# Half-row loads of x, weights split two steps ahead, and taps inside the pairs in a one-layer hybrid trunk

## The chip, the core and the metric

One core of one Trainium2 chip runs the kernel. The metric is the device time of one execution in microseconds; lower is better. A core has a matrix engine (TensorE, in the rows PE, with its weight loads as PEld), VectorE (DVE), ScalarE (ACT), GpSimd (POOL) and SyncE (SP); DMAs are issued here from the queues of SP, GpSimd and ScalarE.

## What is computed

One layer over 1024 tokens of width 1024, all in float32:

```python
h = rms_norm(x, norm_g)
z = einsum('bsd,de->bse', h, w_in)                     # 1024 -> 11 * 1024
u = gelu(z_u); v = layer_norm(gelu(z_v))
br_a = gmlp_spatial_gate(u, v, w_s, b_s) * silu(z_ga)  # per chunk of 128 tokens
c = causal_depthwise_conv(z_a * sigmoid(z_b), conv_w)  # 31 taps
br_b = silu(layer_norm(c)) * silu(z_gb)
att = memory_cross_attention(z_q, rms_norm(mem), w_kv) # 4 heads, 256 memory tokens
br_c = att * silu(z_gc)
proj = einsum('bsnw,nwd->bsnd', [br_a, br_b, br_c], w_branch)
merged = sum over n of sigmoid(z_merge)[n] * proj[n]
out = rms_norm(x + einsum('bsd,de->bse', merged, w_out), final_norm_g)
```

## The kernel before

Every product is made of three: each operand is split into a high part (a cast on ScalarE, `A.copy`, L74) and a low part (a subtraction on VectorE, L75), and high*high, high*low and low*high are summed. So a weight costs TensorE time only after both have run on it. Tiles come from pools: `slots` holds 39 buffers of 4 KB per partition, the tag `op` six buffers for operands (`NOP`), `raw` three for weights as loaded.

A planner puts the instructions of each engine in an order, from the program's order and readiness; what goes through `keep` (and `raw_load` with `pin`) stays behind the instruction written before it on its engine. All loads of the opening go through `sload` (L177), which is kept so, on SP's queue.

The stages, in order of time:

- **Memory keys** (L258 to L310): eight chunks of the key weights (`kload`, three in flight), with the gains of the memory rows. `x_load(k)` (L190) brings the transposed row tile k of x, 512 KB, into its slot, all eight between chunk 2 here and chunk 0 of the next stage; `x_gain` (L244) reads only its first half. `diagonals` (L112) spreads per-token factors onto diagonal tiles that `spread` multiplies by ones; it takes `op` buffers.
- **Memory values** (L336 to L370): eight chunks (`v_load`), product L352. At chunk 1, `xt_load` brings four (`NXT`) token-major tiles of x, at chunks 5 and 6 `squares` sums one each and loads another. The values go to DRAM through GpSimd's queue (`vdram`).
- **The v projection** (L387 to L437), product L400: 16 weight chunks, loaded with `raw_load(wv[...], True)`; `squares(6)` stands behind chunk 0; `x_norm` and `combine` prepare both halves of x in spare time.
- **Pairs** (L687 to L716): for p of 4 and ten blocks i of the input projection, `pair` (L454) makes two output tiles out of seven half-size products L446 (Strassen-Winograd), each 12 instructions of 512 columns. Its operands are made by `operand`. The last two products of a pair are written as `pend` and run inside the next. Behind each pair `pump(PUMP[i])` writes 3 to 8 taps of the depthwise convolution (L544), a chain of 30 per channel tile on VectorE. `spump` writes sums of weights.
- **First merge** (L860 to L870): `merge(0, d)` for eight steps d; `proj` (L753) has 48 products L763 in eight k steps, with the attention between them, and `pump(PUMPA)`. Weights of the first two steps are split ahead (`NRDY`), others by `weights(n, d)` when their step begins.
- **Second merge** (L879 to L924): the same for branch C, while branch B's convolution is centred (`center`), its rstd taken (`conv_rstd`, 8 products of one column, L897, then a chain of small steps), spread over the channels (L130) and applied (`normed`, which also loads branch B's gates through GpSimd's queue, `sgb`). `conv_rstd` stands ahead of step 4, the spread at its k step 4.
- **Branch B and output** (L927 to L1143): two more Strassen-Winograd products (L963), and the final norm: `ypart` adds, squares and multiplies by the norm's gain, `yend` (L1090) takes the rstd, scales and stores each tile of 128 tokens.

Of the kernel before, what the change touches and what calls it, by code (L numbers as in the profile page):

```python
# [16 lines left out]
P = 128  # L17
# [4 lines left out]
H = 512  # L22
# [17 lines left out]
def trunk(ctx, tc, xt, x, memt, wf, wv, wkf, wkv, mem, wbr, wb1, wo, wst, bs, cols, fng, out):  # L40
# [71 lines left out]
    def diagonals(r, n):  # L112
        rh = small.tile([P, n], F32R, tag=f"rh{n}", name=nm("rh"))
        rl = small.tile([P, n], F32R, tag=f"rl{n}", name=nm("rl"))
        split(r, rh, rl)
        groups = []
        for i0 in range(0, n, 4):
            w = min(4, n - i0)
            dg = wpool.tile([P, 2, 4, P], F32R, tag="op", name=nm("dg"), bufs=NOP)
            for j, v in enumerate((rh, rl)):  # L120
                V.tensor_tensor(dg[:, j, :w, :], ident[:, None, :].broadcast_to([P, w, P]),
                                f(v)[:, i0:i0 + w, None].broadcast_to([P, w, P]), ALU.mult)
            groups.append((i0, w, dg))
        return groups
# [65 lines left out]
    def x_load(k):  # L190
        xr[k] = slot(s="xr")
        sload(xr[k], xt[k])
# [65 lines left out]
    for g in range(2):  # L258
        pst = [bank() for _ in range(4)]
        for j in range(4):  # L260
# [23 lines left out]
            if i < MT:  # L284
                sload(mtok[i], mem[i * P:(i + 1) * P, :])
            elif i < 4:
                x_load(i - 2)
            elif i == 4:
                x_load(2)
                x_load(3)  # L290
            else:
                v_load(i - 5)
                x_load(i - 1)
# [42 lines left out]
    for hf in range(2):  # L336
        pst = [bank() for _ in range(MT)]
        for c in range(4):
# [3 lines left out]
            if i == 0:  # L342
                x_load(7)
# [13 lines left out]
            if i == 1:  # L357
                for t in range(NXT):
                    xt_load(t)
            if i in (5, 6):  # L360
                squares(1)
        vv = [slot(F32R, (P, 2, MT, HD), "v") for _ in range(2)]
# [91 lines left out]
    def pair(blk, p, consume, last=False):  # L454
# [9 lines left out]
        A.copy(p1, x)  # L464
        if pend:
            pend.pop(0)()
        ca, cb = slot(s="ca"), slot(s="cb")

        def second():
            o12 = operand(a12)  # L470
            prod(z, o12, B[1][0], True, True)
            V.tensor_tensor(ca[:, :H], z, p1, ALU.add)

# [4 lines left out]
        if pend:  # L478
            pend.pop(0)()
        os2 = operand(s2)  # L480
        prod(x, os2, T2, False, True)
        u2 = half("u2")
        A.copy(u2, x)  # L483
        os1 = operand(s1)
        y = bank("y")
        prod(y, os1, T1, True, True)
        os3 = operand(s3)
# [5 lines left out]
        V.tensor_tensor(cb[:, H:], y, u3, ALU.add)  # L493
        o22 = operand(a22)
# [192 lines left out]
    for p in range(4):  # L687
        for i, (blk, fn, then) in enumerate((
# [16 lines left out]
            if i >= SP0:  # L705
                spump(1)
            if (p, i) == (3, 9):
                for e in range(NPRE):
                    branch_tile(e, bra[e])
            pair(blk, p, kept(fn, then), (p, i) == (3, 9))  # L710
# [3 lines left out]
            pump(PUMP[i] if (p, i) != (3, 8) else 1)  # L714
# [38 lines left out]
    def proj(n, d, xhi, xlo, between=None):  # L753
        hi, lo = ready.pop((n, d), None) or weights(n, d)
        fetch(order.index((n, d)) + 1 + NFETCH)
        ps = acc()
        for k in range(KT):
            if k == 4 and between:
                between()
# [7 lines left out]
    def merge(n, d, between=None):  # L767
        g = load(gdram[n][d], s="gate")
        ps = proj(n, d, bhi, blo, between)
# [109 lines left out]
    for d in range(NRDY):  # L879
        ready[2, d] = weights(2, d)  # L880
# [29 lines left out]
    for d in range(KT):  # L910
        if d == 4:
            conv_rstd()
            crb = slot(s="crb")
        g = merge(2, d, (lambda: spread(crs, crb, misc)) if d == 4 else None)
# [5 lines left out]
        for e in range(3 * d, min(3 * d + 3, KT)):  # L920
            center(e)
        if d >= 4:
# [153 lines left out]
    def ypart(i, c, x0, x1, p, last, n=0, o=ALU.add):  # L1076
        v = ys[i][:, x0:x1]
        V.tensor_tensor(v, v, p, o)
        if last:
# [3 lines left out]
            V.tensor_tensor(v, v, fg[:, x0:x1], ALU.mult)  # L1083
            if last == 1:
                V.tensor_scalar(fa[:, i, 0:1], fs[:, i, q:q + 1], 1.0 / D, RMS_EPS, ALU.mult, ALU.add)
            else:
                d = fa[:, i, 1:2] if last == 2 else fa[:, i, 0:1]
                V.tensor_scalar(d, fs[:, i, q:q + 1], 1.0 / D, fa[:, i, 0:1], ALU.mult, ALU.add)

    def yend(i):  # L1090
# [9 lines left out]
        if w:  # L1100
# [61 lines left out]
NXT = 4  # L1162
# [58 lines left out]
```

## Time and profile before

| | us |
|---|---|
| median of three runs | 1336.66 (1334.66 to 1337.34) |
| profiled execution | 1337.65 |
| its span, first to last instruction | 1335.9 |
| TensorE busy | 1310.3 (98%) |
| VectorE busy | 1084.9 (81%) |
| ScalarE busy | 614.6 (46%) |
| mean granted clock of TensorE | 0.991 |

A granted clock of 1.00 is 2.4 GHz, 0.50 is 1.2 GHz. A row of the timeline has the start of an instruction (or of several alike, xN), its length, engine, line, output<-input, and in brackets how long the engine was idle before it and what ended that. Lines are those of the kernel; where a helper issues an instruction, its line is the helper's.

### The profile page before, as it was taken

Reading aid. Unit: us, or ns where it says so; the run is one execution under the profiler, and the core shown is the slowest. Engines: PE = TensorE matmul, PEld = TensorE weight load, DVE = VectorE, ACT = ScalarE, POOL = GpSimd, SP = SyncE. Lnnn points to the kernel's source line nnn. Section 1 sums busy time; section 2 is a strip of 40 time slices with the busy share of each in tenths; the row PEclk is TensorE's granted clock in tenths of the full one; section 3 lists DMA queues with packets and bytes.
Section 4 is the critical chain, followed back from the end, with each engine's and each line's share of the span. In section 5 each row is a group of like instructions: output and inputs, shape, how many; then the busy total and the mean of one; then the engine's idle time right before and its main releaser. Section 6 shows DMA issues by size and latency. Waiting matters only on the chain.

```text
span 1335.9 us, 16332 instructions
## 1 busy us (share of the span) xinstructions
PE 1310.3 (98%) x6010; PEld 1090.8 (82%) x6010; DVE 1084.9 (81%) x1467; ACT 614.6 (46%) x1012; POOL 114.4 (9%) x194
## 2 busy tenths in 40 slices
PE   9899999999999999999999999999999998999997
PEld 8688888888888888888788888888888887888886
DVE  5779758989969987986996997797698486985886
ACT  6557645445435435444444344444543552443245
POOL 0100000121001111001112001101000010000000
PEclk9899999999999999999999999999999998999999
DMA  8944323786335686426668417545755355455933
GB/s 321 407 143 158 117 80 110 236 267 210 130 110 148 214 236 228 143 79 169 225 210 255 126 48 189 189 159 199 273 189 173 127 189 173 168 211 202 405 133 126
DMA packets 80864, 249.74 MB, mean 187 GB/s; under 512 B 8208, under 2 KB 17936, under 8 KB 80784
## 3 DMA queue, kind: packets, MB, share of 16 engines
q1 hardware_dynamic: 54400, 153.44, 33.0%
q0 software_dynamic: 26096, 94.91, 23.2%
q8 instruction: 47, 0.77, 0.2%
q10 hardware_dynamic: 288, 0.35, 0.1%
q14 instruction: 33, 0.27, 0.1%
HBM read 176.84 MB, written 68.16 MB: 183 GB/s over the span
## 4 chain that ended last, share of the span: by engine, by line
PE 87%; DMA 5%; DVE 4%; ACT 2%; issue 1%; SPq 0%; POOL 0%; DVEq 0%; POOLq 0%; ACTq 0%
PE x L446 29%; PE y L446 15%; PE acc L763 13%; PE acc L963 10%; PE z L446 8%; PE b L400 7%; PE acc L801 2%; PE acc L837 2%; DVE conv L544 1%; DMA kvraw<-in_wkv 1%; DMA xr<-in_xt 1%; DMA raw<-in_wf 1%; PE b L352 1%; PE sp L621 1%; DMA ws<-in_wo 1%
## 5 line engine op out<-in xcount | busy, mean ns | idle before, releaser
L446 PE MATMUL x<-T,op 128*128 128x512 f32 x1440 | 347.8, 390 | 0.9 <-ACT u L483 0.7
L446 PEld LDWEIGHTS x<-T,op 128*128 128x128 f32 x1440 | 269.6, 188 | 58.5 <-ACT u L483 2.8
L74 ACT CAST op<-sum 128x512 fp32r<-128x512 f32 x160 | 99.4, 622 | 115.6 <-PE z L446 51.5
L544 DVE SCALAR_TENSOR_TENSOR conv<-cb,col,conv 128x994 f32<-128x994 f32 (+14 forms) x120 | 151.6, 1263 | 0.8 <-ACT conv L540 0.5
L75 DVE TENSOR_TENSOR op<-sum,op 128x512 fp32r<-128x512 f32 x160 | 108.4, 683 | 22.2 <-ACT op L74 22.1
L446 PE MATMUL z<-B,op 128*128 128x512 f32 x480 | 115.6, 389 | 1.6 <-DVE op L75 1.6
L446 PE MATMUL x<-B,op 128*128 128x512 f32 x480 | 115.5, 389 | 0.0
L446 PE MATMUL y<-B,op 128*128 128x512 f32 x480 | 115.5, 389 | 0.0
L446 PE MATMUL y<-T,op 128*128 128x512 f32 x480 | 115.3, 389 | 0.0
L544 DVE SCALAR_TENSOR_TENSOR conv<-ca,col,conv 128x994 f32<-128x994 f32 (+14 forms) x90 | 113.4, 1260 | 0.4
L74 ACT CAST op<-raw 128x512 fp32r<-128x512 f32 x120 | 74.4, 621 | 77.3 <-PE y L446 75.9
L446 PEld LDWEIGHTS z<-B,op 128*128 128x128 f32 x480 | 90.0, 188 | 20.7 <-DVE op L75 2.0
L446 PEld LDWEIGHTS y<-B,op 128*128 128x128 f32 x480 | 90.1, 188 | 18.7
L446 PEld LDWEIGHTS x<-B,op 128*128 128x128 f32 x480 | 90.1, 188 | 18.7
L446 PEld LDWEIGHTS y<-T,op 128*128 128x128 f32 x480 | 90.1, 188 | 18.7
L75 DVE TENSOR_TENSOR op<-raw,op 128x512 fp32r<-128x512 f32 x120 | 82.2, 685 | 26.3 <-ACT op L74 26.1
L763 PE MATMUL acc<-bhi,whi 128*128 128x512 f32 x256 | 81.1, 399 | 4.4 <-ACT whi L74 3.6
L763 PE MATMUL acc<-bhi,wlo 128*128 128x512 f32 x256 | 80.7, 396 | 0.7 <-DVE wlo L75 0.7
L763 PE MATMUL acc<-blo,whi 128*128 128x512 f32 x256 | 80.5, 396 | 0.0
L963 PE MATMUL acc<-q,sw 128*128 128x512 f32 x288 | 65.4, 389 | 0.0
L963 PEld LDWEIGHTS acc<-q,sw 128*128 128x128 f32 x288 | 54.1, 188 | 11.2
L490 ACT COPY u<-x 128x512 f32<-128x512 f32 x40 | 23.6, 589 | 82.1 <-PE x L446 82.1
(265 smaller groups left out, 2171.3 us busy)
## 6 DMA issues: line engine op xcount, KB each, us to landing
raw<-in_wf SPq DMA_DIRECT2D x80, 512.0 KB, 3.7
sw<-sw SPq DMA_DIRECT2D x40, 512.0 KB, 7.8
sw<-wsh POOLq DMA_DIRECT2D x20, 512.0 KB, 3.5
sw<-ws POOLq DMA_DIRECT2D x20, 512.0 KB, 5.7
raw<-in_wv SPq DMA_DIRECT2D x16, 512.0 KB, 3.5
raw<-in_wbr SPq DMA_DIRECT2D x16, 512.0 KB, 5.5
gate<-g SPq DMA_DIRECT2D x16, 512.0 KB, 4.8
ws<-in_wb POOLq DMA_DIRECT2D x14, 512.0 KB, 5.9
```

The costliest lines, as they stand in the source:

```text
L74: A.copy(hi, src)
L75: V.tensor_tensor(lo, src, f(hi), ALU.subtract)
L352: T.matmul(pst[m], a[k][:, ms], w[:, ws], start=(k == 0 and j == 0), stop=(k == KT - 1 and j == 2))
L400: T.matmul(pst[t], q[:, a, ts_], w[:, ws], start=(k == 0 and j == 0), stop=(k == KT - 1 and j == 2))
L446: T.matmul(ps, w[:, a, ks], m[k][:, b, :], start=(start and k == 0 and j == 0), stop=(stop and k == 3 and j == 2), skip_group_check=not start)
L490: A.copy(u3, x)
L544: V.scalar_tensor_tensor(out=a[:, PAD - j:], in0=g[:, :n], scalar=col[:, cw + j:cw + j + 1], in1=a[:, PAD - j:], op0=ALU.mult, op1=ALU.add)
L621: T.matmul(ps[:, t * P:(t + 1) * P], va[:, 4 * hf + t, :], ws[:, i, :], start=True, stop=True)
L763: T.matmul(ps[:, hf, :], w[:, ks], m[k][:, hf * H:(hf + 1) * H], start=(k == 0 and j == 0), stop=(k == KT - 1 and j == 2))
L801: T.matmul(ps[:, i, :], q[a][:, d, i * P:(i + 1) * P], kk[:, b, d, :], start=(d == 0 and j == 0), stop=(d == 1 and j == 2))
L837: T.matmul(ps[:, d, :], vv[:, a, m, d * P:(d + 1) * P], p2[b][:, m, :], start=(m == 0 and j == 0), stop=(m == MT - 1 and j == 2))
L963: T.matmul(ps[t], a[k][i][:, ts_], w[k][n], start=(start and k == 0 and j == 0), stop=(k == 3 and j == 2), skip_group_check=not start)
```

## The change

- x in halves: `x_load` brings the first half of a row tile (256 KB), two at each of key chunks 2 to 4, one at 5 and 6. The second halves are eight loads behind value chunk 7.
- The token-major tiles are loaded one at each of value chunks 2 to 6 (`NXT` is 5), and one more behind each of the squares at chunks 5 and 6.
- `diagonals` takes its tiles from `slots`, not from `op`.
- `pair` calls `fill` at seven points (`NFILL`: behind the copy of p1, each of the two `pend`, z + p1, the copy of u2, the product with T1, and y + u3), each writing its share of `PUMP[i]` taps; the last two pairs write two taps each, where they wrote one and seven.
- `merge` writes the split of the weights two steps on behind its products, so `proj` finds its weights always ready; `conv_rstd` is called at k step 2 of step 4, and the spread stands behind that step.
- In the final norm the sum of squares is scaled ahead of the multiply by the gain; for the last tile columns 512 to 640 get gain and rstd in one instruction.

```diff
@@ diagonals
-            dg = wpool.tile([P, 2, 4, P], F32R, tag="op", name=nm("dg"), bufs=NOP)
+            dg = slot(F32R, (P, 2, 4, P), "dg")
@@ x_load
-        xr[k] = slot(s="xr")
-        sload(xr[k], xt[k])
+        if k < KT:
+            xr[k] = slot(s="xr")
+            sload(xr[k][:, :H], xt[k][:, :H])
@@ key chunks
-            elif i < 4:
-                x_load(i - 2)
-            elif i == 4:
-                x_load(2)
-                x_load(3)
+            elif i < 5:
+                x_load(2 * i - 4)
+                x_load(2 * i - 3)
             else:
                 v_load(i - 5)
-                x_load(i - 1)
+                x_load(i + 1)
@@ value chunks
-            if i == 0:
-                x_load(7)
...
-            if i == 1:
-                for t in range(NXT):
-                    xt_load(t)
+            if 2 <= i < 2 + NXT:
+                xt_load(i - 2)
             if i in (5, 6):
                 squares(1)
+            if i == 7:
+                for k in range(KT):
+                    sload(xr[k][:, H:], xt[k][:, H:])
@@ pair
-    def pair(blk, p, consume, last=False):
+    def pair(blk, p, consume, fill=lambda: None, last=False):
...
         A.copy(p1, x)
+        fill()
         if pend:
             pend.pop(0)()
+        fill()
@@ pairs
+            share = iter(range(NFILL))
+
+            def fill():
+                k = next(share)
+                n = PUMP[i] if 10 * p + i < 38 else 2
+                pump(n * (k + 1) // NFILL - n * k // NFILL)
+
...
-            pump(PUMP[i] if (p, i) != (3, 8) else 1)
@@ proj, merge
-        hi, lo = ready.pop((n, d), None) or weights(n, d)
+        hi, lo = ready.pop((n, d))
...
-            if k == 4 and between:
+            if k == at and between:
...
-        ps = proj(n, d, bhi, blo, between)
+        ps = proj(n, d, bhi, blo, between, at)
+        i = order.index((n, d)) + NRDY
+        if i < len(order):
+            ready[order[i]] = weights(*order[i])
@@ second merge
-    for d in range(NRDY):
-        ready[2, d] = weights(2, d)
...
-        if d == 4:
-            conv_rstd()
-            crb = slot(s="crb")
-        g = merge(2, d, (lambda: spread(crs, crb, misc)) if d == 4 else None)
+        g = merge(2, d, conv_rstd if d == 4 else None, 2)
...
+        if d == 4:
+            crb = slot(s="crb")
+            spread(crs, crb, misc)
@@ ypart
-            V.tensor_tensor(v, v, fg[:, x0:x1], ALU.mult)
             if last == 1:
...
+            w = max(x0, 640) if i == 3 and c else x0
+            V.tensor_tensor(ys[i][:, w:x1], ys[i][:, w:x1], fg[:, w:x1], ALU.mult)
@@ yend
-        if w:
+        if i == 3:
+            V.tensor_scalar(v[:, :H], v[:, :H], rr, None, ALU.mult)
+            V.scalar_tensor_tensor(out=v[:, H:w], in0=v[:, H:w], scalar=rr, in1=fg[:, H:w], op0=ALU.mult, op1=ALU.mult)
+            nc.sync.dma_start(out=out[rows, :w], in_=v[:, :w])
+        elif w:
@@ constants
-NXT = 4
+NFILL = 7
+NXT = 5
```

## Rows read from the trace of the kernel before

**Rows 1.** engines' busy us (page, section 1); a group of taps (section 5)

```profile
PE 1310.3 (98%) x6010; PEld 1090.8 (82%) x6010; DVE 1084.9 (81%) x1467; ACT 614.6 (46%) x1012; POOL 114.4 (9%) x194
...
L544 DVE SCALAR_TENSOR_TENSOR conv<-cb,col,conv 128x994 f32<-128x994 f32 (+14 forms) x120 | 151.6, 1263 | 0.8 <-ACT conv L540 0.5
```

**Rows 2.** the chain that ended last: start us, length us, what (whole span)

```profile
54.07 11.02 PE b L352 x36
...
65.09 16.32 PE b L400 x72
...
153.09 2.72 PE x L446 x12
```

**Rows 3.** waits of TensorE, longest first: us in total, times, longest (whole span)

```profile
PE b L352 <- ACT whi L74: 5.5, 1, 5.5
...
PE acc L763 <- ACT whi L74: 3.6, 1, 3.6
```

**Rows 4.** stretches: us; PE, PEld, DVE, ACT, POOL busy (count); clock, DMA share, GB/s

```profile
6.00:8.00 2.00, 2.00 (x18) 1.94 (x17) 1.09 (x2) 0.59 (x2) 0.00 (x0) 1.00 0.88 339
...
20.00:24.00 4.00, 3.52 (x29) 3.31 (x28) 3.60 (x8) 3.70 (x7) 0.00 (x0) 1.00 0.36 97
...
48.00:54.00 6.00, 0.57 (x3) 0.13 (x1) 4.26 (x8) 3.52 (x7) 0.00 (x0) 0.88 1.02 418
...
54.00:59.40 5.40, 5.33 (x12) 3.96 (x13) 5.40 (x7) 3.86 (x7) 1.07 (x2) 0.50 1.03 413
```

**Rows 5.** SP's queue in the opening: start us, length, line, transfer, how many

```profile
31.51 4.16 SPq L178 DMA_DIRECT2D xtok<-in_x  x4
...
37.91 3.79 SPq L178 DMA_DIRECT2D kvraw<-in_wkv  x3
```

**Rows 6.** stretches: the pairs, the rstd of the second merge, the normalising

```profile
153.00:934.50 781.50, 779.08 (x3496) 645.66 (x3495) 664.13 (x854) 352.69 (x552) 90.53 (x145) 1.00 0.56 172
...
1124.50:1134.50 10.00, 8.12 (x18) 5.96 (x19) 4.84 (x7) 2.05 (x3) 0.00 (x0) 0.50 0.59 188
...
1137.80:1169.00 31.20, 31.20 (x139) 25.80 (x139) 30.22 (x28) 14.35 (x15) 2.16 (x4) 1.00 0.53 180
```

**Rows 7.** timeline around the rstd: start us, length, engine, line [idle before]

```profile
1120.24 1.84 PE L897 MATMUL acc<-ones,csq 128*128 128x1 f32 x16
...
1124.56 1.99 ACT L74 CAST whi<-raw 128x1024 fp32r<-128x1024 f32 x2
...
1126.58 0.68 DVE L121 TENSOR_TENSOR dg<-ident,rl 128x512 fp32r<-128x512 f32 x1
...
1136.01 1.10 PE L130 MATMUL acc<-dg,onesr 128*128 128x512 f32 x4
...
1136.94 0.40 PE L763 MATMUL acc<-bhi,whi 128*128 128x512 f32 x1
```

**Rows 8.** timeline of the value chunks: first product, first store, first weight's cast

```profile
33.40 0.40 PE L352 MATMUL b<-whi,mhi 128*128 128x512 f32 x1
...
54.61 0.53 POOL L149 DMA_DIRECT2D vd<-v  x1 [11.91 <-DVE v L367]
...
59.84 1.05 ACT L74 CAST whi<-raw 128x1024 fp32r<-128x1024 f32 x1 [1.94 <-DMA raw<-in_wv]
```

**Rows 9.** DMA queues from 57 to 63 us: packets, MB, share of 16 engines

```profile
q0 software_dynamic: 259, 1.00, 40.5%
```

**Rows 10.** timeline of VectorE for the last tile

```profile
1329.49 0.68 DVE L1083 TENSOR_TENSOR y<-y,fg 128x512 f32<-128x512 f32 x1
...
1330.09 0.21 DVE L1088 TENSOR_SCALAR fa<-fs,fa 128x1 f32<-128x1 f32 x1
...
1331.40 0.55 DVE L1101 TENSOR_SCALAR y<-y,fr 128x640 f32<-128x640 f32 x1
```

**Rows 11.** GpSimd's queue: first and fourth prefetch of branch B's gates

```profile
1114.12 0.54 POOL L153 DMA_DIRECT2D sgb<-sgb  x1 [30.19 <-DVE csq L146]
...
1123.72 0.54 POOL L153 DMA_DIRECT2D sgb<-sgb  x1 [0.79 <-DVE rs_y L100]
```

More of the change, by code (lines that the diff above doesn't have):

```diff
@@ L472, in second @@
             V.tensor_tensor(ca[:, :H], z, p1, ALU.add)
+            fill()
         V.tensor_tensor(s3, a11, a21, ALU.subtract)
@@ L479, in pair @@
             pend.pop(0)()
+        fill()
         os2 = operand(s2)
@@ L483, in pair @@
         A.copy(u2, x)
+        fill()
         os1 = operand(s1)
@@ L486, in pair @@
         prod(y, os1, T1, True, True)
+        fill()
         os3 = operand(s3)
@@ L493, in pair @@
         V.tensor_tensor(cb[:, H:], y, u3, ALU.add)
+        fill()
         o22 = operand(a22)
@@ L709, in trunk @@
                     branch_tile(e, bra[e])
-            pair(blk, p, kept(fn, then), (p, i) == (3, 9))
+            pair(blk, p, kept(fn, then), fill, (p, i) == (3, 9))
             if i == 3:
@@ L751, in misc, with proj @@
         return acc()[:, 0, :]
-    def proj(n, d, xhi, xlo, between=None):
-        hi, lo = ready.pop((n, d), None) or weights(n, d)
+    def proj(n, d, xhi, xlo, between=None, at=4):
+        hi, lo = ready.pop((n, d))
         fetch(order.index((n, d)) + 1 + NFETCH)
@@ L765, in proj, with merge @@
         return flat(ps)
-    def merge(n, d, between=None):
+    def merge(n, d, between=None, at=4):
         g = load(gdram[n][d], s="gate")
-        ps = proj(n, d, bhi, blo, between)
+        ps = proj(n, d, bhi, blo, between, at)
+        i = order.index((n, d)) + NRDY
+        if i < len(order):
+            ready[order[i]] = weights(*order[i])
         V.tensor_tensor(g, ps, g, ALU.mult)
```

## The prediction

> **What bounds the kernel now.** I read the page's busy times first: TensorE is busy in 1310.3 of 1335.9 us [rows 1], so at most 25.6 us of idling, plus whatever runs at the lower clock, can be had by reordering; no edit here removes a product. A run of 12 products of 512 columns takes 2.72 us, 0.227 us each [rows 2]; this is the price of all TensorE work below. Next I asked what TensorE waits for. Two waits stand out: 5.5 us before a product of the value chunks (L352), and 3.6 us before a branch product (L763), both for a cast on ScalarE [rows 3]. Then I read the stretches around these two waits, the pairs between them, and the end.
>
> **Where each place stands.** The opening is bound by transfers. From 48 to 54 us TensorE is busy 0.57 of 6 us while 418 GB/s arrive; from 54 to 59.4 us it runs at a granted clock of 0.50 [rows 4]: after the idle stretch the clock was at the lower level (1.2 GHz). SP issued four row loads at 31.51 us, before the last three value chunks at 37.91 us [rows 5], so those chunks stood behind them. The four issues are (4.16 - 0.33)/3 = 1.28 us apart: the price of 512 KB on a full queue. The remaining 36 products of L352 took 11.02 us instead of 36 x 0.227 = 8.16, so 2.86 us went to the clock. L400 starts at 65.09 us and is then bound by TensorE [rows 2].
>
> In the pairs TensorE is idle 781.50 - 779.08 = 2.42 us in all [rows 6]. In the second merge, the 16 one-column products of L897 run from 1120.24 to 1122.08 us, the casts of the next two weights wait behind the rstd chain on ScalarE until 1124.56, and the diagonals' products (L130) end at 1136.94 [rows 7]. Most of that stretch also ran at a clock of 0.50 [rows 6].
>
> **Part 1, loads of the opening.** Removed: half of each x row from ahead of the value chunks. Moved: five row loads to value steps 2 to 6, so only two stand before chunk 7; two more are issued at steps 5 and 6 after the squares. Eight half loads of 256 KB stand at step 7, ahead of the first weight load of L400, because the SP queue is kept in program order. The value chunks themselves then arrive well ahead: L352 starts at 33.40 us [rows 8] and has 96 products, so it could end at 33.40 + 21.8 = 55.2 us. But what is late next is the first weight of L400, and nearly all bytes that stood before it still do. Before, it landed at 59.84 us [rows 8]. In front of it now: one more row load (seven, not six), +1.28 us. The halves come in pieces of 2 KB instead of 4 KB. At 6 to 8 us, where such pieces ran among others, 339 GB/s arrived against 418 in the full stretch [rows 4], so six units of 1.28 us could cost up to 23% more, 1.9 us; the queue was not yet full there, so I take 0.4 (0 to 1.9). The stores of the four value outputs share the engines: the first was issued at 54.61 us [rows 8], and from 57 to 63 us the software queue had 40.5% of the engines [rows 9]. Before, some 0.9 MB of the 2.1 MB were moved ahead of the weight (5.2 us x 0.41 x 418 GB/s); now all four stores come earlier: +0.4 to +2.9 us, I take 2.0, since the chunks end some 8 us before the weight. In the other direction, the memory diagonals no longer hold an operand buffer, which may fill the hole at 20 to 24 us, where 97 GB/s arrived [rows 4], 3.1 us of queue lost. The split there followed ScalarE's rsqrt work, which stays, so I take -0.8 (0 to -3.1).
>
> Landing: 59.84 + 1.28 + 0.4 + 2.0 - 0.8 = 62.7 us. The cast takes 1.05 us [rows 8], and the third product waits a further 0.4 us or so for the low part: 64.2. TensorE will have idled some 8 us by then, longer than the stretch that brought the clock down before, so I charge the same 2.9 us again: an equivalent start at 67.1 against 65.09. **Opening: +2.0 us**, between -5.5 (hole filled, nothing extra, clock kept) and +5.2.
>
> The Trainium skill ("DMA: Bandwidth & Descriptors", Specifications) puts the size from which a transfer runs at line rate at 512 B, so by it the 2 KB pieces cost nothing and the sum would be 0.4 us lower. The 339 GB/s above do not settle it, and no run here shows 2 KB pieces on a full queue.
>
> **Part 2, taps between products.** Removed: the block of 3 to 8 taps behind each pair. Added: the same taps, one or two at a time, at seven points. A tap is 1.26 us of VectorE [rows 1]. Gain is bounded by the 2.42 us of idling above. The cost side has no row, since the order of VectorE's queue is made by a planner from the program order; one pair late by one tap costs 1.26 us at most. I take -1.0 (-2.4 to +3). Some six taps move from the last pairs into the first merge, 6 x 1.26 = 7.6 us of VectorE. Their result is the input of the token mean, which is not wanted before the second merge; hidden. If that cover were gone, it would be those 7.6 us.
>
> **Part 3, weights two steps ahead and the rstd.** Removed: the order in which the weights' casts queue behind the rstd chain. Moved: L897 goes behind 12 of the 48 products of step 4, and L130 behind all 48. Between them 36 x 0.227 = 8.2 us of products cover the chain, which took from 1122.1 to 1127.3, 5.2 us [rows 7]. What remains of the stretch from 1120.24 to 1136.94 us (16.70): L897 1.84, 24 products 5.44, L130 0.93, together 8.21. **-8.5 us**, the clock's share included, since no idling is left to bring it down. What is late next is the normalising behind the rstd: VectorE is busy 30.22 of 31.20 us there [rows 6], and TensorE's work from L130's end to the next stage (three steps of 48, 32.6 us, less 1.1 for the copy) leaves 31.5. That just fits; a slip of up to 2 us is taken into the range (-8.5 to -6.5). The token mean's split now needs two operand buffers while three weights hold six, so it waits for the first merge's last product; the centring that follows has some 5 us to spare before L897.
>
> **Part 4, the end.** For the last tile, the sum's scaling (1330.09) stands behind the multiply of 0.68 us that begins at 1329.49 [rows 10]. Taken ahead, it saves 0.6; the multiply, now 384 columns (some 0.5 us), then delays the reciprocal by 0.2, and two instructions instead of the 0.55 us one add 0.15 in front of the SP store, but not of the ACT store. **-0.45 us** (-0.6 to 0).
>
> **Sum.** +2.0 - 1.0 - 8.5 - 0.45 = -7.95 us. The profiled execution took 1337.65 us (span 1335.9 and 1.75 around it), giving 1329.7; the median of the runs is 1.0 lower, giving **1328.7 us**.
>
> **Rivals.** A: the diagonals take slots that are not there. In the second merge 32 of 39 slots are held (8 merged, 16 branch halves, 8 conv tiles). The other seven hold two gates, the spread rstd and four prefetched gate tiles of branch B; the first and fourth of these were issued at 1114.12 and 1123.72 us, each as a slot came free [rows 11]. Two diagonals more make nine for seven. If the prefetches win, a diagonal waits for a gate's release a step later, normalising starts about a step (10.9 us) later, and the next stage waits some 6 us: 1334.7. For it: the prefetches took every freed slot. Against it: the diagonals come earlier in program order.
>
> B: the first weight of L400 comes early enough (hole filled, stores in the shadow): opening -5 instead of +2, 1321.7. Against it: 418 GB/s in that stretch and no byte less in front.
>
> C, slower: taps at seven points stand ahead of operand splits in VectorE's strictly ordered queue. For it: VectorE is busy 664.13 of 781.50 us in the pairs [rows 6], so a split displaced by a tap is made up slowly. With 40 pairs and 7.95 + 2.7 us to lose (2.7 is 0.2%), it decides from 0.27 us a pair; at 0.4 us a pair the gain of 1.0 is replaced by a loss of 16: 1345.7. Against it: the operand buffers let VectorE run up to six operands ahead.
>
> D: the planner reorders so that little changes: casts still queue behind the rstd chain and part 3 is worth nothing: 1337.
>
> **How the numbers follow.** Forecast as summed 0.53; A 0.20; B 0.14; C 0.07; D 0.06. The forecast's own bounds: -16.9 to +1.7 if all ends met, realistically 1323 to 1333. The range takes in A's time and most of B: 1320.5 to 1335.5. A measurement of this kernel can tell about 0.2%, 2.7 us, from no change. Faster by more than that (below 1334.0): forecast 0.52, B 0.14, a third of A 0.07, part of the rest 0.07: 0.80. Within: 0.13. Slower: 0.07.
>
> **What would show it.** Right: no product of L352 waits, yet L400 starts between 62 and 66 us behind a cast that waits for its weight's load, with a lower clock there; between L897 and L130 TensorE has no gap and the clock stays at 1.00; the stretch from the first L446 to the last stays near 781 us. Wrong: L400 starts before 60 us (B); L130 stands a step later, or the first L963 waits for VectorE (A); waits of L446 for splits above 5 us in sum (C); casts of L763 still behind the rstd chain (D).

## The result

The changed kernel takes 1329.09 us (median of four runs, 1328.36 to 1329.95) where the kernel before takes 1336.93 beside it: a ratio of 0.9945, 95% interval 0.9928 to 0.9962. That is 7.8 us less. The forecast was 1328.7 us, 8.0 less than the median it started from. The profiled execution has a span of 1328.2 us (1335.9 before).

The sum came out right, but three of its terms did not: the opening, the pairs and the first merge. The table gives the first product of each stage on TensorE in the timelines of the two kernels (a chain of waits gives most of these points up to 0.2 us later). Each column is one profiled execution; the changed kernel's was the slowest of its four.

| stage | before | after | difference | forecast |
|---|---|---|---|---|
| opening, to the first pair | 152.92 | 156.98 | +4.06 | +2.0 |
| pairs | 782.93 | 779.22 | -3.71 | -1.0 |
| first merge | 139.70 | 140.30 | +0.60 | 0 |
| second merge | 99.49 | 91.00 | -8.49 | -8.5 |
| output products and end | 160.89 | 160.74 | -0.15 | -0.45 |

New line numbers: the value products are L349 (L352 before), the v projection L399 (L400), the pairs L445 (L446), the merges L775 (L763), the one-column products L910 (L897).

The longest waits of TensorE in the changed kernel, over the whole span (total us, times, longest):

```profile
PE b L399 <- ACT whi L74: 11.0, 1, 11.0
...
PE acc L775 <- DVE ca L508: 0.9, 1, 0.9
...
PE acc L816 <- DMA k<-kd: 0.4, 1, 0.4
```

Against [rows 3], both waits of before are gone: the value products wait no more, and no merge step waits for a cast. In their place stands one wait of 11.0 us in front of the v projection. Its chain, in order of time (start, length, what):

```profile
28.94 13.04 DMA kvraw<-in_wkv
...
41.99 14.68 DMA xr<-in_xt
...
56.69 8.10 DMA raw<-in_wv
...
64.86 1.05 ACT whi L74
...
65.96 1.22 PE b L399 x2
...
67.22 18.24 PE b L399 x70
```

The eight half loads of x are on the chain from 41.99 to 56.67 us, then the first v weight, which lands at 64.8. The 70 products from 67.22 on take 18.24 us, and at 0.227 us they would take 15.9. The stretches around it (stretch; its length, busy time of PE, PEld, DVE, ACT and POOL; clock, DMA share, GB/s):

```profile
20.00:24.00 4.00, 3.72 (x30) 3.51 (x30) 2.83 (x8) 3.32 (x5) 0.00 (x0) 1.00 0.80 272
48.00:54.00 6.00, 6.00 (x28) 4.99 (x27) 4.01 (x6) 1.64 (x4) 0.10 (x1) 1.00 1.03 420
54.00:60.00 6.00, 0.92 (x5) 0.42 (x3) 1.84 (x4) 3.35 (x8) 1.06 (x2) 0.83 1.05 398
60.00:66.00 6.00, 0.04 (x1) 0.04 (x1) 0.06 (x1) 1.04 (x1) 0.00 (x0) 0.50 1.03 419
66.00:72.00 6.00, 5.96 (x14) 4.23 (x15) 5.55 (x11) 2.27 (x4) 0.00 (x0) 0.53 0.58 182
```

Compare [rows 4]: from 48 to 54 us TensorE is now busy throughout, where it had 0.57 of 6 us. The idle stretch has moved behind the value products, to 55 to 66 us, with the DMA engines busy throughout (398 and 419 GB/s), and the lower clock has moved with it. Around the rstd (start, length, engine, line), the first product behind the one-column products in the kernel before, then the changed kernel:

```profile
1125.66 1.22 PE L763 MATMUL acc<-bhi,whi 128*128 128x512 f32 x2 [3.57 <-ACT whi L74]
...
1123.90 1.84 PE L910 MATMUL acc<-ones,csq 128*128 128x1 f32 x16
1125.60 0.72 PE L775 MATMUL acc<-bhi,whi 128*128 128x512 f32 x2
...
1133.45 0.61 PE L775 MATMUL acc<-bhi,wlo 128*128 128x512 f32 x2
1133.90 1.09 PE L130 MATMUL acc<-dg,onesr 128*128 128x512 f32 x4
1134.83 0.62 PE L775 MATMUL acc<-bhi,whi 128*128 128x512 f32 x2
```

No gap is left between the one-column products and the spread, and the granted clock is 1.00 from 1123 to 1135 us (before: 3.57 us idle and, behind it, the lower clock of [rows 6]).

### The profile page after: what moved, and what is told of

Read it like the earlier page. It is cut to its first block, busy times and chain, and to the rows that moved or that the text cites. A ratio compares the mean times of both kernels' runs of the same rounds, so it can differ in the third digit from the quotient of the medians.

```text
span 1328.2 us, 16325 instructions
## 1 busy us (share of the span) xinstructions
PE 1304.8 (98%) x6010; PEld 1087.9 (82%) x6010; DVE 1088.4 (82%) x1468; ACT 616.8 (46%) x1012; POOL 114.7 (9%) x194
## 4 chain that ended last, share of the span: by engine, by line
PE 91%; DMA 5%; ACT 1%; DVE 1%; issue 1%; SPq 0%; POOL 0%; ACTq 0%; POOLq 0%
PE x L445 33%; PE y L445 16%; PE acc L775 12%; PE acc L976 10%; PE z L445 8%; PE b L399 7%; DMA xr<-in_xt 2%; PE acc L816 2%; PE acc L852 1%; PE sp L627 1%; DMA kvraw<-in_wkv 1%; DMA k<-kd 1%; DMA raw<-in_wv 1%; DMA mtok<-in_mem 1%; PE acc L837 0%
## 5 line engine op out<-in xcount | busy, mean ns | idle before, releaser
L445 PE MATMUL x<-T,op 128*128 128x512 f32 x1440 | 347.3, 390 | 0.0
L445 PEld LDWEIGHTS x<-T,op 128*128 128x128 f32 x1440 | 269.9, 188 | 56.4 <-ACT u L486 0.5
L445 PE MATMUL x<-B,op 128*128 128x512 f32 x480 | 115.5, 389 | 0.0
L445 PE MATMUL z<-B,op 128*128 128x512 f32 x480 | 115.3, 389 | 0.0
L445 PE MATMUL y<-T,op 128*128 128x512 f32 x480 | 115.3, 389 | 0.0
L445 PE MATMUL y<-B,op 128*128 128x512 f32 x480 | 115.3, 389 | 0.0
L445 PEld LDWEIGHTS y<-B,op 128*128 128x128 f32 x480 | 90.1, 188 | 18.7
L445 PEld LDWEIGHTS x<-B,op 128*128 128x128 f32 x480 | 90.1, 188 | 18.7
L445 PEld LDWEIGHTS z<-B,op 128*128 128x128 f32 x480 | 90.1, 188 | 18.7
L445 PEld LDWEIGHTS y<-T,op 128*128 128x128 f32 x480 | 90.1, 188 | 18.7
L775 PE MATMUL acc<-bhi,whi 128*128 128x512 f32 x256 | 79.7, 393 | 0.9 <-DVE ca L508 0.9
L775 PE MATMUL acc<-bhi,wlo 128*128 128x512 f32 x256 | 79.3, 390 | 0.0
L775 PE MATMUL acc<-blo,whi 128*128 128x512 f32 x256 | 79.2, 390 | 0.0
```

The costliest lines, as they stand in the source:

```text
L445: T.matmul(ps, w[:, a, ks], m[k][:, b, :], start=(start and k == 0 and j == 0), stop=(stop and k == 3 and j == 2), skip_group_check=not start)
L775: T.matmul(ps[:, hf, :], w[:, ks], m[k][:, hf * H:(hf + 1) * H], start=(k == 0 and j == 0), stop=(k == KT - 1 and j == 2))
```

## The experiments

The theory to be tested: the second merge gains 8.5 us from the order of the weights and of the root; the taps give the shorter pairs; the opening costs 4 us because transfers stand in front of the first v weight, part of it through the lower clock. In each diff, the minus lines are the changed kernel's unless it says otherwise, and three dots stand for lines left out. The expectations count the second merge by a chain of waits (1078.97 to 1167.66 us in the changed kernel, 88.7); that is 2.3 us less than the table's 91.00, which the texts below go by.

**u_open**, the opening of before in the changed kernel:

```
-            elif i < 5:
-                x_load(2 * i - 4)
-                x_load(2 * i - 3)
+            elif i < 4:
+                x_load(i - 2)
...
-            if 2 <= i < 2 + NXT:
-                xt_load(i - 2)
+            if i == 1:
+                for t in range(NXT):
+                    xt_load(t)
...
-                for k in range(KT):
-                    sload(xr[k][:, H:], xt[k][:, H:])
```

> The changed kernel with the opening of before put back: x loaded whole, four row loads in one place, the eighth x load in the value chunks. The diagonals stay in slots. Theory: the opening of the change costs about 4 us (first product of the pairs at 157.2 us instead of 153.1) and gives nothing later, so this kernel reaches 1325 us, 4 us under the changed kernel, with the pairs starting at 152 to 154 us and their stretch still near 779 us. Rival: the shorter pairs come from where the opening leaves the loads (the first pairs start later, with their weights long there); then the pairs take 781 to 783 us here and the time is 1328 to 1329. Second rival: moving the diagonals to slots alone gives the value chunks an early chunk; then the pairs start before 152 us.

Measured: 1324.37 us (ratio to before 0.990, 0.9884 to 0.9915). The first pair starts at 151.75 us and the pairs take 779.25. So the opening of the change costs 5.2 us beside the diagonals in slots (3.1 to 5.2, since one and the same opening moves by 2 us between executions, as the last section shows), and the shorter pairs do not come from it. The second rival's sign came true as well, by 0.25 us: with the opening of before, the diagonals in slots alone bring the first pair from 152.92 to 151.75, before 152 us.

**u_taps**, the taps in one batch behind each pair:

```
-            pair(blk, p, kept(fn, then), fill, (p, i) == (3, 9))
+            pair(blk, p, kept(fn, then), (p, i) == (3, 9))
...
+            pump(PUMP[i] if (p, i) != (3, 8) else 1)
```

> The changed kernel with the taps put back behind each pair in one batch, and the batch sizes of before. Theory: the taps are what shortened the pairs, so their stretch goes back from 779.0 to 782.5 or 783 us and the time to 1332.5 us; TensorE shows once more some short waits in mid-pair on VectorE's operand splits. Rival: the pairs gained by something else (a different start, which shifts pairs against loads); then their stretch stays at 779 to 780 us and the time at 1329 to 1330 us.

Measured: 1332.52 us (0.996, 0.9947 to 0.9972); the pairs take 783.22 us. The theory stands. One of its stalls, on TensorE and on VectorE:

```profile
665.12 1.07 PE L445 MATMUL y<-B,op 128*128 128x512 f32 x4
667.76 2.58 PE L445 MATMUL z<-B,op 128*128 128x512 f32 x10 [1.58 <-DVE op L75]
...
663.54 1.26 DVE L543 SCALAR_TENSOR_TENSOR conv<-ca,col,conv 128x1004 f32<-128x1004 f32 x1
664.71 1.22 DVE L75 TENSOR_TENSOR ws<-ws,wsh 128x1024 fp32r<-128x1024 f32 x1
665.85 1.26 DVE L543 SCALAR_TENSOR_TENSOR conv<-ca,col,conv 128x1005 f32<-128x1005 f32 x1
667.02 0.68 DVE L75 TENSOR_TENSOR op<-raw,op 128x512 fp32r<-128x512 f32 x1
```

VectorE works without a break through taps (L543) and a weight sum's split of 1.22 us; the operand's split comes behind both, at 667.02, and the next products wait for it.

**u_merge**, weights and root in the order of before:

```
-        ps = proj(n, d, bhi, blo, between, at)
-        i = order.index((n, d)) + NRDY
-        if i < len(order):
-            ready[order[i]] = weights(*order[i])
+        ps = proj(n, d, bhi, blo, between)
...
-        g = merge(2, d, conv_rstd if d == 4 else None, 2)
+        if d == 4:
+            conv_rstd()
+            crb = slot(s="crb")
+        g = merge(2, d, (lambda: spread(crs, crb, misc)) if d == 4 else None)
```

> The changed kernel with the weights of the merges split where before split them, and the row sum of squares, its root and its spread all ahead of the fifth gate step's products. Theory: the second merge goes back from 88.7 us (1078.97 to 1167.66) to 96 to 97.5 us, with the granted clock at 0.50 for some 10 us of it, and the time to 1337 or 1337.5 us. Rival: with the diagonals in slots the root no longer waits for a place, so part of the 8.5 us came from there; then the second merge takes 91 to 94 us and the time is 1332 to 1334.

Measured: 1329.13 us (0.9933, 0.992 to 0.9945), the second merge 90.96 us (88.7 by the expectation's count). Both expectations fall in their numbers, though the rival looked in the right place: the part to which I had given the 8.5 us can be taken out for nothing. What is left of the change in this place is one line, the diagonals in slots. Weight casts and the root on ScalarE in u_merge:

```profile
1103.64 1.03 ACT L74 CAST whi<-raw 128x1024 fp32r<-128x1024 f32 x1
1111.59 1.03 ACT L74 CAST whi<-raw 128x1024 fp32r<-128x1024 f32 x1
1120.44 1.05 ACT L74 CAST whi<-raw 128x1024 fp32r<-128x1024 f32 x1 [7.82 <-PE acc L775]
1122.80 0.21 ACT L99 ACTIVATE rs_s<-ms 128x8 f32<-128x8 f32 x1
```

Three casts stand ahead of the root (1122.80). In the kernel before there was none between 1090.30 and the two at 1124.56 [rows 7], though the program has the same order in both, and ScalarE was idle for 9.79 us ahead of the root:

```profile
1090.30 1.06 ACT L74 CAST whi<-raw 128x1024 fp32r<-128x1024 f32 x1 [4.01 <-PE acc L763]
...
1122.32 0.21 ACT L99 ACTIVATE rs_s<-ms 128x8 f32<-128x8 f32 x1 [9.79 <-DVE ms L109]
```

The weights themselves were there: the loads of merge weights ahead of TensorE's gap were issued at 1109.43 us at the latest, and each landed within 5.2 us.

**b_dg**, the kernel before with that one line (minus is before):

```
-            dg = wpool.tile([P, 2, 4, P], F32R, tag="op", name=nm("dg"), bufs=NOP)
+            dg = slot(F32R, (P, 2, 4, P), "dg")
```

> The kernel before with one line changed: the diagonals take places among the slots and no longer among the six operand buffers. Taking the merge part out of the changed kernel (u_merge) did not cost anything, so one of two things is true. Theory: in the kernel before, the diagonals of the row root stand in front of the fifth gate step's weights in the line for the operand buffers, so that these weights cannot be cast before the root is done; with the diagonals elsewhere the casts go ahead, the second merge falls from 97 us to 89 and, with an opening about 1.2 us shorter (as in u_open), the time to 1326 to 1328 us. Rival: the taps between the products or the new opening freed ScalarE and VectorE for the earlier cast; then the second merge keeps its 97 us here and the time is 1335 to 1337.

Measured: 1326.3 us (0.9912, 0.9897 to 0.9927). The first pair starts at 151.15 us and the second merge takes 90.98. One line takes 11.3 us off the span (8.5 in the second merge, 1.8 in the opening, 1.1 in the pairs, for which no cause is shown), where the whole change takes 7.7. ScalarE casts ahead of the root again:

```profile
1100.34 1.04 ACT L74 CAST whi<-raw 128x1024 fp32r<-128x1024 f32 x1
1108.28 1.04 ACT L74 CAST whi<-raw 128x1024 fp32r<-128x1024 f32 x1
1117.14 1.05 ACT L74 CAST whi<-raw 128x1024 fp32r<-128x1024 f32 x1 [7.82 <-PE acc L763]
1119.50 0.21 ACT L99 ACTIVATE rs_s<-ms 128x8 f32<-128x8 f32 x1
```

The reading that fits before, u_merge, b_dg and d_op (the runs show which edit removes the wait; no trace shows the handing out of buffers itself): the six operand buffers are handed out in the order in which the program asks for them. The diagonals ask at `conv_rstd`, ahead of the fifth step's weights, and their place is only filled when the root is done. The Trainium skill ("Perfetto Trace Analysis", Optimization Strategy) reads gaps that repeat on the busiest engine as a possible sign that the next tile can get no buffer. Here a single gap of 3.57 us went when the diagonals left the operand buffers, so a gap that comes once can have that cause too.

**d_op**, the changed kernel with this line as before (the same diff turned round).

> The changed kernel with the diagonals back among the operand buffers. Theory: the weights that are split two steps ahead stand before the diagonals in the line for these buffers, so the merge part does the same work a second time over: the second merge stays at 89 to 90 us, and only the opening is some 1 us longer: 1329 to 1331 us. Rival: the diagonals now wait for operand buffers that the weights split ahead hold, the spread comes late and its products or the next step's weights wait for it: the second merge takes 93 to 97 us, 1333 to 1337 us.

Measured: 1331.96 us (0.9951, 0.9938 to 0.9964); the second merge takes 91.01 us. So the merge part is enough as well: its weights are asked for ahead of the diagonals. Either of the two removes the wait, and both together remove it once. The time is 1 us above the expected range, because the opening got longer than expected: the first value product starts at 36.12 us, not 32.16, and the first pair at 159.58. TensorE waits for a cast in the key products, and that cast comes directly behind the last step of the memory rows' root (`rh`):

```profile
PE b L282 <- ACT whi L74: 3.1, 1, 3.1
...
21.57 0.19 ACT L74 CAST rh<-rs_y 128x2 fp32r<-128x2 f32 x1 [1.02 <-DVE rs_y L104]
21.67 1.04 ACT L74 CAST whi<-kraw 128x1024 fp32r<-128x1024 f32 x1
```

In the changed kernel the cast at this place starts at 18.63 us, ahead of the root (20.97). The same reading fits: the memory rows' diagonals hold back the next key weight. The first pair under the four combinations gives the opening's price without my stage sums: 152.92 (both as before), 151.15 (only the line), 159.58 (only the loads), 156.98 (both). The loads alone cost 6.7 us; the line takes 1.8 us off with the old loads and 2.6 with the new ones. The two with the new loads are single executions, which can be 2 us off.

**u_end**, the end part undone:

```
+            V.tensor_tensor(v, v, fg[:, x0:x1], ALU.mult)
...
-            w = max(x0, 640) if i == 3 and c else x0
-            V.tensor_tensor(ys[i][:, w:x1], ys[i][:, w:x1], fg[:, w:x1], ALU.mult)
...
-        if i == 3:
-            V.tensor_scalar(v[:, :H], v[:, :H], rr, None, ALU.mult)
...
```

> The changed kernel with the gain and the last stores of the final norm as before. Theory: the end part is worth 0.15 to 0.45 us (output stage 160.54 to 160.69 us or more), so 1329.2 to 1329.6 us, within the spread of the runs. Rival: the stores of the last rows hide more; then the output stage is 161.5 us or longer and the time 1330 or more.

Measured: 1328.5 us (0.9929, 0.9914 to 0.9943): as the changed kernel, and 0.7 below the expected range, which its own spread covers (1327.26 to 1330.5). Only the stage can be read: 160.96 us here, 160.89, 160.90 and 161.22 in the other three kernels that have the old end, and 160.39 to 160.86 in the nine that have the new one (mean 160.65 against 160.99). That puts the part at 0.3 us, far inside the spread of the whole time from run to run.

**late_halves**, the second halves of x behind the first v weight:

```
-            if i == 7:
-                for k in range(KT):
-                    sload(xr[k][:, H:], xt[k][:, H:])
...
                 if th == 0:
+                    if i < 4:
+                        for k in (2 * i, 2 * i + 1):
+                            sload(xr[k][:, H:], xt[k][:, H:])
```

> The changed kernel with one thing moved: the loads of the second halves of x go out two at a time behind the first four chunks of the v projection's first half, behind the first v weight, instead of all eight ahead of it. Theory: the eight half loads (2 MB at some 419 GB/s, 5 us) in front of the first v weight are what delays the v projection; without them that weight is there at 57 to 60 us instead of 64.8 and the clock falls little or not at all, so the v projection starts at 56 to 61 us and the pairs at 147 to 151 us: 1320 to 1324 us, under both kernels. Rival: the row loads, the stores of k and v and the value weights fill the queue by themselves, and the v projection starts at 63 us or later: 1326 to 1329. Second rival: the half loads come too late for the normed x that is written from the third chunk on, and the gain is given back at the second half of the v projection: the pairs still start at 155 us or later.

Measured: 1322.45 us (0.9885, 0.9871 to 0.9898). The v projection starts at 59.69 us and the first pair at 150.19; the theory stands, though the clock still fell (granted 0.79 from 54 to 60 us and 0.64 from 60 to 66). The wait left there is on ScalarE: the weight's cast starts at 58.59 us, directly behind two row squares (55.80 and 57.55).

**late_vstores**, the changed kernel with the last v stores behind the second v weight:

```
-        for hh in range(2):
-            store(vdram[hf * 2 + hh], f(vv[hh]))
+        if hf == 0:
+            for hh in range(2):
+                store(vdram[hh], f(vv[hh]))
...
                     elif i == 1:
+                        for hh in range(2):
+                            sload(vdram[2 + hh], f(vv[hh]))
```

> The changed kernel with the stores of the last two value outputs (1 MB) issued on SP's queue, behind the second v weight, and no longer on GpSimd's ahead of the first one's landing. Theory: the term of the opening that the prediction sized too small is the stores: the last two start at 56.3 and 58.0 us and had 0.99 MB moved by 64.8 us, when the first v weight landed; at 419 GB/s that is 2.4 us. So the weight lands at 62 to 63 us, the v projection starts at 63 to 64 us, the pairs at 154 to 155 instead of 157, and the time is 1326.5 to 1327.5 us. Rival: it is the order and the eight half loads alone, the software queue's share being taken from transfers behind the weight; then the start stays within 0.5 us and the time at 1328.7 to 1329.5.

Measured: 1326.81 us (0.993, 0.9916 to 0.9943). The first v weight is cast at 62.19 us, against 64.86 in the changed kernel:

```profile
62.19 1.04 ACT L74 CAST whi<-raw 128x1024 fp32r<-128x1024 f32 x1 [4.04 <-DMA raw<-in_wv]
```

Four other executions of an unchanged opening (u_taps, u_merge, u_end, warm_hole) cast it at 63.06 to 65.21 us, mean with the changed kernel 64.35, so the stores account for 2.2 us by that mean, and for 0.9 to 3.0 by the single executions. The theory's 2.4 stands within that. The Trainium skill ("DMA: Bandwidth & Descriptors", Queues, rings and completion order) says that each DMA engine goes round the queues that have work for it. The run agrees that they share: stores on GpSimd's queue delay a weight that SP issued beside them, and moving them behind it in SP's queue gave the time back.

**warm_hole**, the changed kernel with products in the idle stretch:

```
+    warm = bank("warm")
+    for i in range(NHOLE):
+        T.matmul(warm, onesr, xg[0][:, 0, :], start=True, stop=True)
...
+NHOLE = 42
```

> The changed kernel with 42 products of 512 columns, whose result nobody reads, on TensorE between the last value product and the first v product (42 x 0.227 = 9.5 of the 11.1 us in which it stood idle). Theory: the v projection takes 91.0 us in the changed kernel and 88.0 in those without the idle stretch because it begins at the lower clock; with TensorE kept at work it starts at the same 66 us, takes 88.0 to 88.5 us, and the time is 1326 to 1327 us. Rival: the 3 us belong to the transfers that follow the late weight; then it still takes 90.5 us or more and the time is 1329.

Measured: 1326.64 us (0.9923, 0.9911 to 0.9936). The v projection starts at 66.31 us, no earlier, and takes 88.14 us instead of 91.02. The stretches, to be compared with those of the changed kernel above:

```profile
60.00:66.00 6.00, 5.92 (x26) 4.44 (x24) 0.00 (x0) 0.79 (x1) 0.00 (x0) 1.00 1.03 413
66.00:72.00 6.00, 5.68 (x25) 4.72 (x26) 4.92 (x9) 2.57 (x5) 0.00 (x0) 1.00 0.70 240
```

The granted clock is 1.00 (2.4 GHz) in both, where it was 0.50 and 0.53 (1.2 GHz for nearly all of the time). So 2.9 us of the opening were the clock's (2.6 to 3.2 against the four executions of the unchanged opening, whose v projection takes 90.71 to 91.32 us).

**taps_only**, the kernel before with the taps part alone (the diff of u_taps turned round).

> The kernel before with only the taps written between the products of a pair. Theory: the part is worth the same alone as in the changed kernel: the stretch of the pairs falls from 782.9 us to 779.2 (no stall of 0.5 us or more between two products), the rest stays, and the time is 1333 to 1334.5 us. Rival: part of the shorter pairs needs the other parts; then the stretch is 780.5 to 782 us and the time 1335 to 1336.5.

Measured: 1334.61 us (0.9986, 0.9977 to 0.9995), 0.1 above the expected range. The pairs take 779.21 us, so this part needs no other. The first merge takes 140.38 us instead of 139.70, a cost that belongs to this part too: in u_taps, without it, the first merge takes 139.76.

**weight_first**, late_halves with the first two v weights loaded ahead of the last four row loads, and the row root one chunk later (minus is late_halves):

```
+            if i in (4, 6):
+                wvr.append(raw_load(wv[i // 2 - 2], True))
...
-                hi, lo = wchunk(None, raw_load(wv[ch * 4 + c], True))
+                hi, lo = wchunk(None, wvr.pop(0) if wvr else raw_load(wv[ch * 4 + c], True))
...
-                    if i < 4:
+                    if 1 <= i < 5:
...
-                    elif i == 2:
+                    elif i == 3:
                         rb = slot(s="rb")
                         spread(xdg, rb, bank)
```

> The kernel of late_halves with the first two v weights loaded in the value chunks, ahead of the last four of the eight row loads, and the row squares, their root and its spread one chunk of the v projection later. Nothing is left out. Theory: the v projection began at 59.7 us in late_halves because its first weight was cast at 58.6, behind row squares on ScalarE that waited for their loads; with the weight ahead of them it begins at 55 to 56 us, right behind the last value product (55.2), without the lower clock, takes 88 us as in the kernel before and not 90.5, and the pairs begin at 143 to 144.5 us: 1314.5 to 1316.5 us. Rival: the bytes in front of the v projection are the bound, so the later row loads or half loads make its second half wait, and the pairs begin at 147 us or later: 1319 us or more. Second rival: TensorE's clock falls at this place whatever stands there; then the stretch stays at 90.5 us and the time is 1317.5 to 1319.

Measured: 1315.89 us (0.9832, 0.9817 to 0.9847), 1.7% under the kernel before. The first v weight's cast and its chain from the value products to the first pair:

```profile
50.68 1.05 ACT L74 CAST whi<-raw 128x1024 fp32r<-128x1024 f32 x1 [0.21 <-DMA raw<-in_wv]
...
44.87 11.11 PE b L354 x49
55.98 10.88 PE b L403 x48
...
78.70 65.31 PE b L403 x288
144.01 2.72 PE x L454 x12
```

The weight is cast at 50.68 us, while value products (L354) still run. The v projection (L403) follows them at once and the chain is TensorE alone; the granted clock stays at 1.00, with 420 GB/s arriving from 48 to 54 us. The first pair starts at 143.84 us, 13 us earlier than in the changed kernel, without a byte less to load. Of these 13, about 3 are the clock's: the v projection takes 88.03 us instead of 91.02.

## Why the prediction was right, and where it was not

**Opening, +2.0 forecast, +4.06 measured.** What the prediction said would come late next did: the value products wait no longer, the v projection starts at 65.96 us (62 to 66 forecast) behind a cast that waits for its load, at a lower clock. The clock's 2.9 us is what warm_hole measured. The term that was mis-sized most is the stores. Bytes per queue up to the landing of the first v weight, in before (to 59.84 us) and after (to 64.80 us); packets, MB, share:

```profile
q1 hardware_dynamic: 5608, 18.88, 82.4%
q0 software_dynamic: 654, 2.42, 9.9%
...
q1 hardware_dynamic: 6959, 19.60, 81.0%
q0 software_dynamic: 1122, 4.14, 15.6%
```

The software queue had moved 1.72 MB more by then, which at 419 GB/s is 4.1 us where the prediction took 2.0 (0.4 to 2.9). It had put 0.9 MB of value stores ahead of the weight in the kernel before, by applying the share of 57 to 63 us [rows 9] from 54.61 us on; with 2.10 MB of key stores taken off, the queue's count leaves 0.32 MB. In four more executions of this opening (u_taps, u_merge, u_end, warm_hole) the queue had moved 3.87 to 4.10 MB by that landing, so the term is 3.5 to 4.1 us in all five. The loads' 0.72 MB are 1.7 us, of which the one row more (0.52 MB) is 1.25 (1.28 forecast).

The 2 KB pieces do cost something. The packets from 54.0 to 59.4 us, most of them the half loads (some 2.1 KB each without the 141 smallest), and the stretch behind them:

```profile
DMA packets 1148, 2.14 MB, mean 396 GB/s; under 512 B 141, under 2 KB 141, under 8 KB 1148
...
59.40:64.80 5.40, 0.00 (x0) 0.00 (x0) 0.00 (x0) 0.00 (x0) 0.00 (x0) 0.50 1.03 420
```

From 54.0 to 59.4 us 396 GB/s arrived, against 420 from 48 to 54 us and from 59.4 to 64.8, where nearly all pieces are of 4 KB. The lower rate costs 0.3 us for these 2.1 MB, an estimate from the two rates. The forecast of 0.4 was near, and for the early half loads too low: from 24 to 30 us 347 GB/s arrived, and 414 in u_open with whole rows and the engines as busy. The Trainium skill ("DMA: Bandwidth & Descriptors", Specifications) gives line rate from 512 B on. The trace differs, by these 6% at 2 KB, and decides here.

What is left to the landing, 4.96 - 4.1 - 1.7 - 0.3 = -1.1 us, is the net of the other stretches (-0.8 forecast). The filled hole alone is worth -1.7 (272 GB/s from 20 to 24 us, 97 before), and stretches such as that from 24 to 30 us (347, 377 before) took part of it back. It is the diagonals' place that filled the hole: 272 and 309 GB/s in u_open and b_dg, 155 in d_op. The prediction's reason for a small gain, that the split stays behind ScalarE's root, failed (18.63 against 20.97 us, see d_op), so this term came out near by chance.

How far the opening was missed is not sharp: the four kernels with this opening start the first pair at 156.3 us on average, +3.4 and not +4.06, and u_end's single execution at 154.86 is +1.9. Rival B, which had the first weight early enough, fell.

**Pairs, -1.0 forecast, -3.7 measured, outside the bound of 2.4.** The direction and the cause hold (u_taps, taps_only). The bound failed: the idle time between two products is not what a stall costs. In the stall shown above the row says 1.58 us; the products start at 665.12 and every 0.227 us after, so the next was due at 666.03 and came at 667.76, 1.73 us late. In the kernel before, four stalls in mid-pair add up to 3.0 us by starts; the rest of the 3.7 is in delays of 0.2 us or less. The sign "near 781 us" from the first product to the last was not met either (777.95). The size differs between executions with the old batches: 783.22 in u_taps and 781.88 in b_dg, so the gain is 2.7 to 4.0. Rival C (splits pushed behind taps) did not occur: no pair waits for VectorE in the changed kernel.

**Six taps hidden in the first merge, 0 forecast, +0.6 measured.** This step failed too. No tap changed stage (30 stand in the first merge in both), but those of the last tile begin at 972.21 us instead of 959.12. VectorE's time is covered as forecast; what was missed stands on GpSimd's queue, behind the tile's store and its accumulation. The load of the last head's keys in before and after (that this order makes it late is read from the rows, not tested alone):

```profile
1023.18 0.91 POOL L549 DMA_DIRECT2D csum<-conv  x1
1023.90 0.75 POOL L153 DMA_DIRECT2D k<-kd  x1
...
1032.79 0.92 POOL L555 DMA_DIRECT2D csum<-conv  x1
1033.36 0.90 POOL L153 DMA_DIRECT2D k<-kd  x1
```

It is issued 9.5 us later, and the attention products (L816) wait 0.4 us for it, 0.54 between starts.

**Second merge, -8.5 forecast, -8.49 measured.** The size is right: the 16.70 us of [rows 7] lost what the sum said, and the spread no longer waits. The cause as written was too narrow. The casts did stand behind the root's chain, but, by the reading above, because of the place of the diagonals among the operand buffers, which the prediction named for the opening and for rival A and not here. So it gave the gain to the larger edit. b_dg and u_merge show the one line enough, d_op shows the larger edit enough. Rival A went the other way: the diagonals got their slots, and the third prefetch came at 1134.83 us, once the spread was done. Rival D fell with the gap.

**End, -0.45 forecast, -0.15 between the two profiles and -0.3 over all kernels.** This is inside its range of -0.6 to 0.

The sum was right in part by chance, since errors of opposite sign cancelled: by the two profiles the opening was 2.1 us too low, the first merge 0.6, the end 0.3, and the pairs 2.7 too high. Two slips in the working weigh 0.1 us each and change nothing: 23% of six units of 1.28 us are 1.8 us, not 1.9, and the lower ends add up to -17.0, not -16.9.

## What to carry to other kernels

When a cast or split comes late with its input long landed, ask which tile stands ahead of it in the line for its buffer, and give a tile that is filled late a pool of its own: here one line took 11.3 us off the span. What matters in a saturated opening is the order of the bytes: put the load that the next stage needs first ahead of those needed a stage later, count stores on other queues as bytes in front of it, and keep TensorE from standing idle there. Undo each part of a change alone: parts that do the same work, as the diagonals' place and the split two steps ahead, do not add.

## What the runs showed of the hardware

- The idle stretch of 11 us in front of the v projection cost 2.9 us more behind it through the clock; 42 products whose result nobody reads gave that back, and the span fell from 1328.2 to 1325.8 us though the stage began no earlier.
- Stores on GpSimd's queue and loads on SP's share the same full rate (413 to 420 GB/s in all): 1 MB of stores moved behind the weight brought it 2.2 us earlier (0.9 to 3.0 by single executions).
- Loads in 2 KB pieces on a full queue arrived at 396 GB/s (54.0 to 59.4 us; 392 to 398 in four more executions of this opening), those in 4 KB pieces at 420.
- The first pair of one and the same opening started at 154.86, 156.53, 156.88 and 156.98 us in four kernels that differ only later, so a stage bound by transfers moves by 2 us from one execution to the next, where the second merge stays within 0.06 us (90.96 to 91.02) in all kernels without the gap.
